# A two-layer mLSTM, GLA and sparse-attention block: matmuls of zeros ahead of the data, a shared first norm, and other buffer counts for the weights

## The chip, the cores and the metric

The kernel runs on one core of a Trainium2 chip. The metric is the device time of one execution in microseconds (us). The engines named below are PE (TensorE, matrix products), DVE (VectorE), ACT (ScalarE), POOL (GpSimd) and SP (SyncE, which here only issues DMAs). PEld is PE's loading of the stationary operand.

## The reference, cut to what matters

One sequence of 512 tokens, width 1024, goes through two layers, all in fp32. A layer normalizes its input, projects it to 9312 columns with one weight matrix, feeds three mixers with the columns, gates their outputs and projects 2048 columns back:

```
p   = split_columns(rmsnorm(x, norm_g) @ w_in)          # [512, 1024] @ [1024, 9312]
hm  = mlstm_chunkwise(silu(conv(p.ml_q, p.ml_k)), p.ml_v, gates) * sigmoid(p.ml_o)
hg  = gla_chunked(p.gla_q, p.gla_k, p.gla_v, decay)     # 4 heads
hd  = dsa_sparse_attention(...)                         # top-128 keys of an index score
y   = concat(norm(hm)*silu(ml_z), norm(hg)*silu(gla_r), hd*silu(dsa_z))
x   = x + y @ w_out                                     # [512, 2048] @ [2048, 1024]
```

Here `rmsnorm(x, g)` is `x * rsqrt(mean(x*x) + 1e-6) * g`.

## The kernel before, in words

**Products in three passes.** Every big product is made of three one-pass matmuls in a rounded fp32 format (fp32r): each operand is split into a high part (rounded) and a low part (the rest), and `mm3` (L516) issues high x high, high x low and low x high. The normalized input is kept as `xhi` and `xlo`, eight tiles of 128 columns for 512 tokens.

**Weights.** The host packs both layers' weights into 178 pieces of 128 x 1024 floats (512 KB), in the order of use. A piece takes three steps: SP loads it as `raw`; ACT copies it to `hi` (fp32r); DVE computes `lo = raw - hi`. All three kinds of tile come from one pool `w` with `W_BUFS` = 11 places, and at most `RAWS` = 3 pieces are loading or unsplit. After the split the raw tile's place is free, so a ready piece holds two places. `make_room` (L460) issues loads, `prepare` (L472) does one step of splitting (first the `lo` of the piece whose `hi` was issued, then the `hi` of the next), and `give_back` (L504) frees a piece that PE has used. A load is booked as landed 4.5 us (`LOAD`) after PE's clock at its issue, and `prepare` does not split a piece whose booked landing lies ahead of that clock. `need` (L488) repeats `prepare` until a piece that is wanted is ready.

**Units.** PE goes through units in a fixed order. A `wide` unit has four pieces and 512 columns: it computes four blocks of 128 tokens, 24 matmuls of 512 columns each (`pn` in the profile). In the first unit of a layer each block `sb` first waits for the norm of its 128 rows of x, and the four blocks run one after another over all four pieces; in other wide units the first two blocks run over all four pieces, and then the last two share each piece. Units `in`, `gqk` and `misc` (two, two and one piece) give transposed results (`pt`); units `out` (four pieces) are the last projection (`pw`).

**Planner.** Each engine runs its instructions in the order in which the program issues them. The order is worked out in Python while the program is built: `Meter` (L164) gives each instruction a cost, `Clock` (L208) keeps a time for each engine, and `Background` (L267) holds generators for all other work (norms, convolutions, scans, attention), each of which yields between steps. After each six or so projection matmuls `tick` (L512) calls `prepare` and then starts steps that are due at PE's clock. These planner times only fix the order; they are no times of the chip.

**The start.** `norm_in` (L614) is the norm of a block of 128 rows: squares and their sum, then two small POOL instructions (`rstd_of`, L412), then the scaled copy `xs` on ACT, then eight transposes on PE in two halves of four (`psx`), after each of which ACT writes four tiles of `xhi` and DVE four tiles of `xlo`. The sum of squares is on DVE for blocks 0, 2 and 3 and on ACT for block 1. The loop after the norm tasks (L657) runs the norm of block 0 by hand: two steps (squares, POOL), `prepare`, one step (`xs`), `prepare`, one step (first half), `prepare`, two steps (second half), `prepare`. PE's planner clock is set to at least 5.0 and 6.5 at the first two.

**Space.** Tiles of 128 x 1024 floats for everything else come from the pool `t4`, with `N_T4` = 11 places.

Of the kernel before, what the change touches and what calls it, by code (L numbers as in the profile page):

```python
# [14 lines left out]
AF = mybir.ActivationFunctionType  # L15
OP = mybir.AluOpType
# [143 lines left out]
def free_size(ap):  # L160
    return math.prod(ap.shape[1:])


class Meter:  # L164


    def __init__(self, engine, name, clock):
        self.engine, self.name, self.clock = engine, name, clock
# [12 lines left out]
    def cost(self, op, args, kw):  # L181
        out = args[0]
        if op == "dma_start":
            return None
        if self.name == "pe":
            if op == "transpose":
                return 0.109
            n, one_pass = free_size(out), kw["rhs"].dtype == F32R
            if one_pass:
                return max(n, 256) / 2210 + 0.002  # L190
            if out.shape[0] == 64:
                return max(n / 950, 0.08)
            return max(4 * n, 256) / 2400 + 0.004
        n = free_size(args[1]) if op == "max" else free_size(out)
        pointers = sum(hasattr(v, "ap") and free_size(v) == 1 for v in (*args[2:], *kw.values()))
        accum = kw.get("accum_out") is not None
        if self.name == "act":
            switch = self.clock.ln != (args[2] == AF.Ln)
            self.clock.ln = args[2] == AF.Ln
            return 0.155 + n / 1138 + 0.09 * pointers + 0.12 * accum + 1.3 * switch  # L200
        if self.name == "dve":
            return 0.15 + n / 945 + 0.06 * min(pointers, 1) + 0.02 * accum
        if kw.get("op") == OP.pow:
            return 0.45 + 0.15 * n
        return 0.1 + n / (510 if op == "tensor_tensor" else 600) + 0.1 * (op == "tensor_tensor")


class Clock:  # L208
# [4 lines left out]
    def __init__(self):  # L213
        self.at = dict(pe=0.0, act=0.0, dve=0.0, pool=0.0, sync=0.0)
        self.now = 0.0
        self.ln = True
        self.written, self.touched = {}, {}
        self.rings = {}

    def begin(self):  # L220
        self.now = self.at["pe"]
# [29 lines left out]
    def book(self, engine, cost, outs, ins):  # L251
        at = self.at
        start = max([at[engine]] + [self.latest(self.written, engine, v) for v in ins]
                    + [self.latest(self.touched, engine, v) for v in outs])
        if cost is None:
            at[engine] = start + self.ISSUE
            end, engine = start + self.DMA, "dma"
        else:
            at[engine] = end = start + cost
        self.now = max(self.now, end)  # L260
        for v in outs:
            self.written.setdefault(v.name, {})[self.box(v)] = end, engine
        for v in outs + ins:
            self.touched.setdefault(v.name, {})[self.box(v)] = end, engine
# [69 lines left out]
def hybrid_kernel(ctx, tc, a, out, dbg=None):  # L334
# [12 lines left out]
            nc.gpsimd.dma_start(dbg[name], ap)  # L347

    ctx.enter_context(tc.manual_schedule())
    N_T4, N_T2 = 11, 19  # L350
    W_BUFS, RAWS, LOAD = 11, 3, 4.5
    const = ctx.enter_context(tc.tile_pool(name="const", bufs=1))
    par = ctx.enter_context(tc.tile_pool(name="par", bufs=2))
    wp = ctx.enter_context(tc.tile_pool(name="wp", bufs=2))
# [6 lines left out]
    def pp(name):  # L361
        t = psp.tile([128, 512], F32, tag="pp", name=name)
        clock.ring("pp", t, 3)
        return t

    def pa(name):
        t = psa.tile([128, 512], F32, tag="pa", name=name)
        clock.ring("pa", t, 5)
        return t

    def t4(name, n=1024, dtype=F32):
        return wk.tile([128, 1024], dtype, tag="t4", name=name, bufs=N_T4)[:, 0:n]
# [4 lines left out]
    def small(name, n=8, bufs=None):  # L377
        return sm.tile([128, n], F32, tag=f"s{n}", name=name, bufs=bufs or {1: 10, 4: 8, 8: 8}[n])

    def blocks(t, b):  # L380
        return t.rearrange("p (b c) -> p b c", b=b)

    xr = const.tile([128, NB, D], F32, name="xr")
# [21 lines left out]
    qzs = [const.tile([128, 2, 64 * NB], F32, name=f"qz{i}") for i in range(2)]  # L405
    for t in qzs:
        for odd, r in enumerate(HALVES):
            nc.gpsimd.memset(t[r, 1 - odd], 0.0)
    lev = const.tile([128, len(LEVELS), 32], U8, name="lev")


    def rstd_of(ss, n, dim, rs, scale=1.0):  # L412
        nc.gpsimd.tensor_scalar(rs, ss, scale / dim, scale * EPS, op0=OP.mult, op1=OP.add)
        nc.gpsimd.tensor_tensor(rs, rs, mhalf[:, :n], op=OP.pow)


    def high_part(ps, hi, gain=None):
        if gain is None:
            nc.scalar.activation(hi, ps, AF.Copy)
        else:  # L420
            for c in range(ps.shape[1]):
                nc.scalar.activation(hi[:, c], ps[:, c], AF.Copy, scale=gain[:, c:c + 1])

    def low_part(ps, hi, lo, gain=None):
        if gain is None:
            nc.vector.tensor_sub(lo, ps, hi.bitcast(F32))
        else:
            for c in range(ps.shape[1]):
                nc.vector.scalar_tensor_tensor(lo[:, c], ps[:, c], gain[:, c:c + 1], hi[:, c].bitcast(F32),
                                               op0=OP.mult, op1=OP.subtract)  # L430
# [16 lines left out]
    units, to_load = [], []  # L447
# [9 lines left out]
    def w_tile(name, dtype):  # L457
        return wp.tile([128, 1024], dtype, tag="w", name=name, bufs=W_BUFS)

    def make_room(most=RAWS):  # L460
        while to_load and state["raw"] < most:
            if state["used"] + 1 > W_BUFS - (2 if any(p.hi is None for p in wanted) or not held else 0):
                break
            p = to_load.pop(0)
            state["used"] += 1
            state["raw"] += 1
            p.raw = w_tile("raw", F32)
            nc.sync.dma_start(p.raw, a["w_pack"][p.layer, p.at])
            p.loaded = clock.at["pe"] + LOAD
            to_split.append(p)  # L470

    def prepare():  # L472
        if half_done:
            p = half_done.pop()
            lo = w_tile("lo", F32R)
            nc.vector.tensor_sub(lo, p.raw, p.hi.bitcast(F32))
            state["used"] -= 1
            state["raw"] -= 1
            p.parts = [[t[:, c:c + p.n] for c in range(0, 1024, p.n)] for t in (p.hi, lo)]
            make_room()  # L480
        if to_split and to_split[0].loaded <= clock.at["pe"] and state["used"] + 2 <= W_BUFS:
            p = to_split.pop(0)
            state["used"] += 2
            p.hi = w_tile("hi", F32R)
            nc.scalar.activation(p.hi, p.raw, AF.Copy)
            half_done.append(p)

    def need(p):  # L488
        while p.parts is None:
            if not half_done:  # L490
                clock.at["pe"] = max(clock.at["pe"], to_split[0].loaded)
            prepare()
        return p.parts
# [16 lines left out]
    bg = Background(clock, N_T2 - 1)  # L510
# [103 lines left out]
    def norm_in(gain, sb, square):  # L614
        xs = t4("xs")
        rs = small("rx", 1)
        if square == "act":
            nc.scalar.activation(xs, xr[:, sb, :], AF.Square, accum_out=rs)
        else:
            nc.vector.tensor_tensor_reduce(xs, xr[:, sb, :], xr[:, sb, :], 1.0, 0.0, op0=OP.mult, op1=OP.add,  # L620
                                           accum_out=rs)
        yield
        rstd_of(rs, 1, D, rs)
        yield
        nc.scalar.activation(xs, xr[:, sb, :], AF.Copy, scale=rs)
        yield
        split = []
        for half in range(2):
            ps = pa("psx")
            for j in range(4):  # L630
                k = 4 * half + j
                nc.tensor.transpose(ps[:, 128 * j:128 * j + 128], xs[:, 128 * k:128 * k + 128], ident)
            d = (slice(None), slice(4 * half, 4 * half + 4), slice(128 * sb, 128 * sb + 128))
            split.append((blocks(ps, 4), xhi[d], xlo[d], gain[:, 4 * half:4 * half + 4]))
            high_part(split[-1][0], split[-1][1], split[-1][3])
            if half:
                low_part(*split[0])
            yield "pe"
        yield
        low_part(*split[1])  # L640
# [6 lines left out]
    params = []  # L647

    def norm_task(layer, sb, ready=0.0):
        return bg.add(norm_in(params[layer][:, 88:96], sb, "act" if sb == 1 else "dve"), "norm", ready)  # L650

    norms = []
    make_room(2)
# [14 lines left out]
    for layer in range(DEPTH):  # L668
# [646 lines left out]
        for n, step in enumerate(PLAN):  # L1315
# [3 lines left out]
            _, name, g0, quarter = step  # L1319
# [32 lines left out]
```

## Time and profile before

| | before |
|---|---|
| time, median of 3 runs | 1228.73 us (1228.69 to 1230.84) |
| profiled execution, its own time | 1227.63 us |
| span of the profiled execution | 1225.9 us |
| PE busy | 1198.3 us (98%) |
| DVE busy | 835.1 us (68%) |
| ACT busy | 600.6 us (49%) |
| POOL busy | 171.0 us (14%) |
| mean granted TensorE clock | 0.996 |
| bytes moved by DMA | 107.70 MB, mean 88 GB/s |

The span runs from the first to the last instruction; the execution's own time is 1.7 us longer. Matmuls overlap in the records: a 512-column fp32r matmul is listed with about 0.40 us, and the next one starts 0.23 us after it. Nearly all instructions stand under line 178, the recorder's call, so rows are told apart by the names of their tiles. The letter q after an engine (SPq) is its instruction queue.

### The profile page before, as it was taken

Reading aid. Unit: us, or ns where it says so; the run is one execution under the profiler, and the core shown is the slowest. Engines: PE = TensorE matmul, PEld = TensorE weight load, DVE = VectorE, ACT = ScalarE, POOL = GpSimd, SP = SyncE. Lnnn points to the kernel's source line nnn. Section 1 sums busy time; section 2 is a strip of 40 time slices with the busy share of each in tenths; the row PEclk is TensorE's granted clock in tenths of the full one; section 3 lists DMA queues with packets and bytes.
Section 4 is the critical chain, followed back from the end, with each engine's and each line's share of the span. In section 5 each row is a group of like instructions: output and inputs, shape, how many; then the busy total and the mean of one; then the engine's idle time right before and its main releaser. Section 6 shows DMA issues by size and latency. Waiting matters only on the chain. (4 is left out here: it accounts for less than half of the span.)

```text
span 1225.9 us, 16513 instructions
## 1 busy us (share of the span) xinstructions
PE 1198.3 (98%) x6004; PEld 970.6 (79%) x6004; DVE 835.1 (68%) x1650; ACT 600.6 (49%) x1334; POOL 171.0 (14%) x309
## 2 busy tenths in 40 slices
PE   6999899999999999999999999999999999999998
PEld 4877687888888887788879777888788888778887
DVE  5477797876777765355555888879867867544644
ACT  6565446554344354652366654474443443555421
POOL 2001221321000010210010023031210000122000
PEclk8999999999999999999999999999999999999999
DMA  5333122212332234132124222222222223233221
GB/s 195 108 98 104 44 92 72 86 61 55 105 108 69 70 119 129 53 112 86 69 70 128 63 86 79 80 73 86 71 70 86 79 85 104 70 112 112 69 82 73
DMA packets 35152, 107.70 MB, mean 88 GB/s; under 512 B 5028, under 2 KB 8388, under 8 KB 35072
## 3 DMA queue, kind: packets, MB, share of 16 engines
q1 hardware_dynamic: 33136, 104.89, 26.5%
q0 software_dynamic: 1200, 1.36, 0.3%
q8 instruction: 47, 0.77, 0.3%
q10 hardware_dynamic: 736, 0.41, 0.1%
q14 instruction: 33, 0.27, 0.1%
HBM read 104.48 MB, written 3.43 MB: 88 GB/s over the span
## 5 line engine op out<-in xcount | busy, mean ns | idle before, releaser
L178 DVE TENSOR_TENSOR lo<-raw,hi 128x1024 fp32r<-128x1024 f32 x178 | 219.1, 1231 | 140.2 <-ACT hi L178 133.5
L178 PE MATMUL pn<-hi,xhi 128*128 128x512 f32 x768 | 313.4, 408 | 0.4 <-ACT xhi L178 0.4
L178 PE MATMUL pn<-lo,xhi 128*128 128x512 f32 x768 | 305.2, 397 | 4.1 <-DVE lo L178 4.1
L178 PE MATMUL pn<-hi,xlo 128*128 128x512 f32 x768 | 304.1, 396 | 0.0
L178 ACT ACTIVATE hi<-raw 128x1024 fp32r<-128x1024 f32 x178 | 188.7, 1060 | 197.9 <-PE pn L178 96.8
L178 PEld LDWEIGHTS pn<-lo,xhi 128*128 128x128 f32 x768 | 145.1, 189 | 37.7 <-DVE lo L178 7.0
L178 PEld LDWEIGHTS pn<-hi,xlo 128*128 128x128 f32 x768 | 144.6, 188 | 35.8 <-DVE xlo L178 1.3
L178 PEld LDWEIGHTS pn<-hi,xhi 128*128 128x128 f32 x768 | 145.1, 189 | 33.2 <-issue 0.8
L178 PE MATMUL pt<-xhi,hi 128*128 128x512 f32 (+1 forms) x400 | 159.1, 398 | 0.0
L178 PE MATMUL pt<-xhi,lo 128*128 128x512 f32 (+1 forms) x400 | 154.6, 387 | 0.0
L178 PE MATMUL pt<-xlo,hi 128*128 128x512 f32 (+1 forms) x400 | 154.5, 386 | 0.0
L178 PE MATMUL pw<-hi,yhi 128*128 128x512 f32 x256 | 102.1, 399 | 0.8 <-DVE zz L178 0.8
L178 PE MATMUL pw<-hi,ylo 128*128 128x512 f32 x256 | 100.0, 391 | 0.0
L178 PE MATMUL pw<-lo,yhi 128*128 128x512 f32 x256 | 99.8, 390 | 0.0
L178 PEld LDWEIGHTS pt<-xhi,hi 128*128 128x128 f32 x400 | 75.2, 188 | 18.0 <-issue 3.9
L178 PEld LDWEIGHTS pt<-xhi,lo 128*128 128x128 f32 x400 | 75.3, 188 | 15.3
L178 PEld LDWEIGHTS pt<-xlo,hi 128*128 128x128 f32 x400 | 75.5, 189 | 12.7
L178 DVE TENSOR_TENSOR xr<-pw,xr 128x512 f32<-128x512 f32 x64 | 44.2, 690 | 58.7 <-PE pw L178 58.7
L178 DVE SCALAR_TENSOR_TENSOR cacc<-cbuf,pv,cacc 128x512 f32<-128x512 f32 x96 | 73.3, 763 | 2.5 <-ACT el L178 0.2
L178 PEld LDWEIGHTS pw<-hi,yhi 128*128 128x128 f32 x256 | 48.1, 188 | 10.5 <-DVE zz L178 1.2
L178 PEld LDWEIGHTS pw<-hi,ylo 128*128 128x128 f32 x256 | 48.0, 188 | 10.3
L178 PEld LDWEIGHTS pw<-lo,yhi 128*128 128x128 f32 x256 | 48.2, 188 | 9.3
(187 smaller groups left out, 1671.0 us busy)
## 6 DMA issues: line engine op xcount, KB each, us to landing
raw<-w_pack SPq DMA_DIRECT2D x178, 512.0 KB, 3.5
xr<-x SPq DMA_DIRECT2D x4, 512.0 KB, 7.3
negm<-negm SPq DMA_DIRECT2D x8, 256.0 KB, 3.7
bs<-skew SPq DMA_DIRECT2D x8, 256.0 KB, 4.0
out_dram<-xr SPq DMA_DIRECT2D x8, 256.0 KB, 2.0
bs<-skew SPq DMA_DIRECT2D x8, 192.0 KB, 4.5
skew<-flat POOLq DMA_DIRECT2D x1, 1280.0 KB, 16.1
bs<-skew SPq DMA_DIRECT2D x8, 128.0 KB, 4.5
```

The source lines that it names most:

```text
L178: return f(*args, **kw)
```

## The change

- Seven matmuls of 256 columns on zeroed data (`qzs[0]`, fp32, 64 rows) are issued to PE before anything else, into a PSUM tile `idle` that nothing reads.
- The norm of block 0 of layer 0 splits the squares: DVE takes columns 0 to 511, ACT columns 512 to 1023, and POOL adds the two sums. The scaled copy `xs` of that block is issued in two halves.
- The `hi` of the very first piece is a DVE copy and no longer an ACT copy.
- The pool `w` has 12 places, at most 2 pieces loading or unsplit; the pool `t4` has 10 places.
- The planner books 0.085 us on PE whenever PE leaves one-pass fp32r matmuls for transposes or other fp32 matmuls.

```diff
             if op == "transpose":
-                return 0.109
+                switch = self.clock.leave()
+                self.clock.projecting = False
+                return 0.109 + switch
             n, one_pass = free_size(out), kw["rhs"].dtype == F32R
+            switch = 0.0 if one_pass else self.clock.leave()
+            self.clock.projecting = one_pass
             if one_pass:
                 return max(n, 256) / 2210 + 0.002
             if out.shape[0] == 64:
-                return max(n / 950, 0.08)
-            return max(4 * n, 256) / 2400 + 0.004
+                return max(n / 950, 0.08) + switch
+            return max(4 * n, 256) / 2400 + 0.004 + switch
...
+        self.projecting = False
...
+    def leave(self):
+        return 0.085 * self.projecting
...
-    N_T4, N_T2 = 11, 19
-    W_BUFS, RAWS, LOAD = 11, 3, 4.5
+    N_T4, N_T2 = 10, 19
+    WARM = 7
+    W_BUFS, RAWS, LOAD = 12, 2, 4.5
...
+    idle = pp("idle")
+    for _ in range(WARM):
+        nc.tensor.matmul(idle[:, 0:256], lhsT=qzs[0][0:64, 1, 0:128], rhs=qzs[0][0:64, 1, :], start=True, stop=True)
...
             p.hi = w_tile("hi", F32R)
-            nc.scalar.activation(p.hi, p.raw, AF.Copy)
+            if p is units[0][1][0]:
+                nc.vector.tensor_copy(p.hi, p.raw)
+            else:
+                nc.scalar.activation(p.hi, p.raw, AF.Copy)
...
-        if square == "act":
+        if square == "both":
+            rs2 = small("rx", 1)
+            l, r = xr[:, sb, 0:512], xr[:, sb, 512:1024]
+            nc.vector.tensor_tensor_reduce(xs[:, 0:512], l, l, 1.0, 0.0, op0=OP.mult, op1=OP.add, accum_out=rs)
+            nc.scalar.activation(xs[:, 512:1024], r, AF.Square, accum_out=rs2)
+            nc.gpsimd.tensor_tensor(rs, rs, rs2, op=OP.add)
+        elif square == "act":
...
-        nc.scalar.activation(xs, xr[:, sb, :], AF.Copy, scale=rs)
+        for c in ((slice(0, 512), slice(512, 1024)) if square == "both" else (slice(0, 1024),)):
+            nc.scalar.activation(xs[:, c], xr[:, sb, c], AF.Copy, scale=rs)
...
-        return bg.add(norm_in(params[layer][:, 88:96], sb, "act" if sb == 1 else "dve"), "norm", ready)
+        return bg.add(norm_in(params[layer][:, 88:96], sb, "act" if sb == 1 else "both" if not (layer or sb) else "dve"), "norm", ready)
```

## Rows read from the trace of the kernel before

**Rows 1.** Page, part 1: engine busy us, share of span, instructions.
```profile
PE 1198.3 (98%) x6004; PEld 970.6 (79%) x6004; DVE 835.1 (68%) x1650; ACT 600.6 (49%) x1334; POOL 171.0 (14%) x309
```
**Rows 2.** Waits of PE: waiter, releaser, us in total, times, longest.
```profile
PE psq L178 <- ACT qn L178: 4.1, 2, 2.2
PE pn L178 <- DVE lo L178: 4.1, 6, 1.9
PE psga L178 <- DVE qz L178: 2.7, 1, 2.7
```
**Rows 3.** Timeline of PE, start: start us, us, engine, line, op, count [idle before].
```profile
8.32 1.97 PE L178 MATMUL psx<-ident,xs 128*128 128x128 f32 x8 [8.32 <-ACT xs L178]
...
12.07 0.42 PE L178 MATMUL pn<-lo,xhi 128*128 128x512 f32 x1
...
16.54 0.40 PE L178 MATMUL pn<-hi,xlo 128*128 128x512 f32 x1
19.80 1.97 PE L178 MATMUL psx<-ident,xs 128*128 128x128 f32 x8 [2.86 <-ACT xs L178]
22.13 0.80 PE L178 MATMUL pn<-hi,xhi 128*128 128x512 f32 x1 [0.36 <-ACT xhi L178]
```
**Rows 4.** Busy time by stretch; the number behind POOL is the granted clock.
```profile
19.80:25.20 5.40, 5.04 (x15) 3.49 (x16) 2.16 (x8) 4.08 (x10) 0.00 (x0) 0.50 0.00 0
```
**Rows 5.** Timeline of DVE, start.
```profile
4.61 1.23 DVE L178 CUSTOM_DVE_ANT_0 xs<-xr 128x1024 f32<-128x1024 f32 x1 [3.44 <-DMA xr<-x]
...
7.26 1.23 DVE L178 TENSOR_TENSOR lo<-raw,hi 128x1024 fp32r<-128x1024 f32 x1 [1.43 <-ACT hi L178]
...
10.65 1.13 DVE L178 SCALAR_TENSOR_TENSOR xlo<-psx,pv,xhi 128x128 fp32r<-128x128 f32 x4 [0.17 <-ACT xhi L178]
...
13.92 1.22 DVE L178 TENSOR_TENSOR lo<-raw,hi 128x1024 fp32r<-128x1024 f32 x1
```
**Rows 6.** Timeline of ACT, start.
```profile
7.13 1.13 ACT L178 ACTIVATE xs<-xr,rx 128x1024 f32<-128x1024 f32 x1
...
9.47 1.14 ACT L178 ACTIVATE xhi<-psx,pv 128x128 fp32r<-128x128 f32 x4 [0.26 <-PE psx L178]
...
14.34 0.24 ACT L178 ACTIVATION_READ_ACCUMULATOR xs<-xr 128x1 f32 x1
17.05 0.85 ACT L178 ACTIVATE zw<-wa 16x256 fp32r<-16x256 f32 x2 [2.47 <-DMA wa<-gla_w_a]
17.91 0.66 ACT L178 ACTIVATE gv<-pn 128x256 f32<-128x256 f32 x2
18.60 3.23 ACT L178 ACTIVATE xs<-xr,rx 128x1024 f32<-128x1024 f32 x3
21.73 2.15 ACT L178 ACTIVATE xhi<-psx,pv 128x128 fp32r<-128x128 f32 x8
...
38.37 1.06 ACT L178 ACTIVATE hi<-raw 128x1024 fp32r<-128x1024 f32 x1 [0.51 <-PE pn L178]
```
**Rows 7.** Timeline of POOL, start.
```profile
1.13 1.33 POOL L178 MEMSET qz<- 64x256 f32 x4
6.02 0.19 POOL L178 TENSOR_SCALAR rx<-rx 128x1 f32<-128x1 f32 x1 [3.56 <-DVE rx L178]
6.29 0.56 POOL L178 TENSOR_TENSOR rx<-rx,mhalf 128x1 f32<-128x1 f32 x1
```
**Rows 8.** Timeline of DVE: a reduction over 512 columns, later in the run.
```profile
488.95 0.69 DVE L178 CUSTOM_DVE_ANT_0 bs<-psl,bs 128x512 f32<-128x512 f32 x1 [5.23 <-POOL bs L178]
```
**Rows 9.** Critical chain: eight fp32 products of 128 columns (16 records).
```profile
1144.84 1.78 PE pod L178 x16
```
**Rows 10.** Timeline of PE: the longest wait for a weight.
```profile
131.91 0.50 PE L178 MATMUL pn<-lo,xhi 128*128 128x512 f32 x1 [1.85 <-DVE lo L178]
```
**Rows 11.** Busy time by stretch, columns as in Rows 4.
```profile
146.00:147.00 1.00, 1.00 (x10) 0.79 (x7) 0.57 (x2) 0.00 (x0) 0.00 (x0) 0.50 0.06 16
494.00:495.00 1.00, 0.58 (x2) 0.28 (x2) 0.00 (x0) 1.00 (x4) 1.00 (x2) 1.00 0.00 0
```

## The prediction

> **What bounds the kernel now.** First the busy shares: PE is busy 98% of the span, every other engine at most 68% [rows 1]. So the time is PE's work plus the stretches in which PE has nothing to do or runs at half rate, and the change can gain only there. Then PE's timeline and its list of waits. At the start PE stands still for 8.32 us, works on the first block of tokens until 16.94, stands still again for 2.86 us and then 0.36 us for the norm of the second block, and gets going at 22.13 [rows 3]; from 19.8 to 25.2 the clock column shows 0.50, the lower of its two levels (1.2 GHz) [rows 4]. All later gaps are small: 4.1 us in six waits for the low part of a weight (the longest 1.85 us), 4.1 us in two waits for the normalized queries and keys, 2.7 us in one wait of the GLA products [rows 2, 10]. The start holds some 11.5 us of idle time, the rest of the run about 12.
>
> **The part that is easy to miss: what the zeros do to the planner.** Seven matmuls go through the recorder, so the planner books them on PE: 0.43 each by the code's formula, from 1.38 (its end of the first memset plus its semaphore cost) to 4.39. The loads of the first four pieces are issued after that in program order, so they are booked as landed at 4.39 + 4.5 = 8.89 instead of 4.5. The four calls of prepare in the start loop come at 5.0, 6.5, about 7.4 and about 8.1 of PE's planner clock (scaled copies booked until 6.77 and 7.47, then two times four transposes), all below 8.89. None of them splits anything; in the kernel before, each did. All splitting starts in need(), after both halves of the first norm. These numbers decide the order only. By them DVE's order becomes: half of the squares, four xlo, hi of piece 0, lo 0, lo 1, four xlo, lo 2, the squares of block 2, lo 3. Before it was: squares, lo 0, lo 1, four xlo, lo 2, four xlo, lo 3, squares of block 2.
>
> **The start in chip time.** The first block of x is usable at 4.61 [rows 5]. DVE's half takes 0.69 as a reduction of 512 columns did [rows 8]; ACT's half I estimate at 0.8, half of 1.13 for 1024 columns plus 0.24 for reading the sum [rows 6]. POOL starts about 0.18 after, as before (5.84 to 6.02), and has three small steps instead of two: 0.27 + 0.27 + 0.56 [rows 7], which ends at 6.7. The first half of xs (0.6) ends at 7.3, the transposes start at 7.4 against 8.32: 0.9 us earlier. The zeros begin behind the first qz memset, at about 1.6 [rows 7]. A 256-column fp32 product costs 0.45 at the full clock (eight of 128 columns took 1.78 [rows 9]) and I estimate 0.9 at the lower level, so seven end between 4.7 and 7.9: in the worst case the transposes start 0.5 late.
>
> Then DVE's chain. Four transposes (0.5 at the full clock, half of 1.97 / 2 [rows 3]) and four xhi (1.14 [rows 6]) put the first xlo at 9.3. From there to the end of lo 3 there are two xlo groups of 1.1, the copy, three lo (0, 1, 2), one squares, and lo 3, each 1.15 to 1.23 [rows 5], and a tiny scale: 2 x 1.1 + 6 x 1.15 + 0.1 = 9.2, so lo 3 ends near 18.5; before it ended at 15.14 [rows 5]. Five matmuls at 0.23 follow, and block 0 ends near 19.75 instead of 16.94: **+2.8**. The hi of piece 0 on DVE does not show in the trace; its bounds are 1.23, the subtraction of the same size, and 0.6, half of it, and I take 1.15 because that row is the nearest. For the copy, the Trainium skill ("VectorE: DVE Perf Modes", The perf-mode tier table) says that an fp32 copy between SBUF tiles runs at twice the rate of a two-input operation. No row here shows one; by that rule the sum of the start would be 0.5 us smaller.
>
> Behind block 0, ACT's order sets when block 1 can begin. Before: zw (which had waited until 17.05 for its DMA), gv, three xs, xhi, and PE's first matmul of block 1 at 22.13, 5.19 after the end of block 0 [rows 3, 6]. After: gv can start at once (-0.85), but with 12 places a fifth piece fits already here (8 held + 2 loading + 2), so its hi (1.06 [rows 6]) goes ahead of the second xs, and zw's 0.85 lands behind it, ahead of the last two xs: about +0.9 in all. So block 1 starts near 25.8: **start +3.7**. Bounds: +2 (short copy, no hi or zw in front) and +5 (block 0's last six matmuls at the lower level, 1.4 more). The zeros do not buy the clock back: PE has little to do from about 8.4 to 11.5 and stands still again before block 1, and a gap of 2.7 us was followed by 0.50 [rows 11] while one of 1.96 was not.
>
> **The weights.** A wide unit holds 8 places. With 11 places and 3 loading nothing more can be split until PE gives the first piece back; with 12 and 2 one piece more is ready. The six waits for lo (4.1 us) are late by 1.85 at most [rows 2, 10], and one piece is at least 24 matmuls x 0.23 = 5.6 us of PE's work: I take all of them as gone, **-4.1**; bounds 0 and -4.1. That a piece loads with one fewer in flight I cost at nothing: DVE's lo hides it, since the next load is issued right there, a piece's worth of work ahead; if that cover went, one wait would cost a landing time.
>
> **The planner's 0.085 and the t4 places.** Both move steps between places, they add no instruction. PE's planner clock runs ahead a little, so steps of ACT and DVE come earlier in program order; the 6.8 us of other waits [rows 2] may shrink or grow. One place fewer in t4 could make a first write wait for the last reader of a place. Cost 0 each; bounds together -4 and +3 (a gap like the longest one more).
>
> **Sum.** Against the profiled execution, 1227.63 (span 1225.9 and 1.7 around it): +3.7 - 4.1 = 1227.2. The median of the runs is 1.1 higher than that execution, so the forecast is **1228.3**, no change that can be measured: a measurement of this kernel can tell about 0.2%, 2.5 us.
>
> **Rivals.**
> *A: the start goes as the words of the change say.* If the splits keep their places in the start loop, DVE copies hi 0 at 6.2, when its raw lands, and its chain ends at 14.0 instead of 15.14; gv's 0.85 less and zw's 0.85 more cancel. Start -1.2, with the weights -5.3: 1223.4. For it: DVE is free from 5.8 to 7.26 [rows 5]. Against it: the planner's 8.89. Chance 0.14.
> *B: the waits in the middle go too.* The GLA wait (2.7) drags a stretch at 0.50 behind it [rows 11], some 3.3 us, so 1.65 more, and the queries and keys cost 4.1 [rows 2]. If half of these 8.4 go: 1228.3 - 4.2 = 1224.1. For it: the planner now knows what leaving the projections costs. Against it: these waits are for DVE and ACT, which the new term does not slow down in its books, so it asks for their results earlier. Chance 0.18.
> *C: slower, because DVE and not the number of places makes lo late.* All six waits are ended by DVE's lo, none by ACT's hi or a load [rows 2, 10]. One more piece split ahead is 1.23 us of DVE work earlier, which pushes the convolutions and the GLA products back by as much, and PE waits there instead. Then the 4.1 stay as other waits and the start's +3.7 stands: 1232.0. It decides as soon as less than 1.2 us of the waits is saved. Chance 0.26.
> The forecast has 0.42, and 1225.8 to 1230.8 for its own range.
>
> **How the numbers follow.** The likeliest case gives the time. Faster by over 0.2%: A, B and a twentieth from the forecast's tail, less a little of B that stays within, 0.35. Slower: most of C and a little of the tail, 0.26. Within: 0.39. The range goes from the far side of A and B, 1222.5, to 1233.0, C with one more microsecond.
>
> **What would show it.** In the profile after: zeros on PE from about 1.6; transposes near 7.4; DVE's lo of piece 0 after the first xlo and lo 3 near 18.5; block 1's first pn near 25.8 (right) or below 21.5 (A). In the list of PE's waits, lo near 0 and psga and psq about as before. The prediction is wrong if block 1 starts before 22.13, if lo still stands at 4 us (C), or if the wait for psga is gone (B).

## The result, and the profile after

The changed kernel takes **1219.13 us** (median of 4 runs, 1218.32 to 1220.31) against 1229.47 for the kernel before in the same session: ratio 0.9915, 95% interval 0.9898 to 0.9933. The prediction was no measurable change (1228.3, range 1222.5 to 1233.0), so it was too slow by 9.2 us. The profiled execution takes 1219.62 with a span of 1217.7, 8.2 us below the span before.

The page's first part after, to hold against [rows 1]:

```profile
PE 1202.5 (99%) x6018; PEld 976.6 (80%) x6018; DVE 832.8 (68%) x1651; ACT 600.2 (49%) x1336; POOL 169.3 (14%) x310
```

PE's waits after (waiter, releaser, us in total, times, longest), to hold against [rows 2]:

```profile
PE psx L178 <- ACT xs L178: 2.7, 1, 2.7
PE pn L178 <- DVE hi L178: 2.2, 1, 2.2
PE pn L178 <- ACT xhi L178: 2.2, 1, 2.2
PE idle L178 <- POOL qz L178: 1.5, 1, 1.5
PE psga L178 <- DVE qz L178: 1.1, 1, 1.1
PE pn L178 <- DVE lo L178: 0.9, 2, 0.5
```

Here idle are the zeros, psx the norm's transposes, pn matmuls of a projection, psga the GLA products, psq the transposes of the normalized queries and keys. The first four lines are all of the start, and so are 0.4 of the 0.9 us for lo (the row at 13.13 below). Of the rest of the run, psq has left the list (4.1 before), lo went from 4.1 to 0.5, psga from 2.7 to 1.1.

PE's timeline at the start, to hold against [rows 3]:

```profile
1.49 6.34 PE L178 MATMUL idle<-qz 64*128 64x256 f32 x14 [1.49 <-POOL qz L178]
7.76 1.97 PE L178 MATMUL psx<-ident,xs 128*128 128x128 f32 x8
11.96 0.77 PE L178 MATMUL pn<-hi,xhi 128*128 128x512 f32 x1 [2.23 <-DVE hi L178]
13.13 0.80 PE L178 MATMUL pn<-lo,xhi 128*128 128x512 f32 x1 [0.40 <-DVE lo L178]
...
20.58 0.40 PE L178 MATMUL pn<-hi,xlo 128*128 128x512 f32 x1
23.70 1.10 PE L178 MATMUL psx<-ident,xs 128*128 128x128 f32 x8 [2.73 <-ACT xs L178]
27.04 0.79 PE L178 MATMUL pn<-hi,xhi 128*128 128x512 f32 x1 [2.23 <-ACT xhi L178]
```

Block 0's last matmul starts at 20.58 (16.54 before), block 1's first at 27.04 (22.13 before). DVE and ACT of the same stretch, to hold against [rows 5, 6]:

```profile
4.62 0.69 DVE L178 CUSTOM_DVE_ANT_0 xs<-xr 128x512 f32<-128x512 f32 x1 [3.45 <-DMA xr<-x]
...
11.13 0.68 DVE L178 CAST hi<-raw 128x1024 fp32r<-128x1024 f32 x1
11.85 2.36 DVE L178 TENSOR_TENSOR lo<-raw,hi 128x1024 fp32r<-128x1024 f32 x2
...
17.50 1.22 DVE L178 TENSOR_TENSOR lo<-raw,hi 128x1024 fp32r<-128x1024 f32 x1
...
21.01 0.66 ACT L178 ACTIVATE gv<-pn 128x256 f32<-128x256 f32 x2 [6.05 <-PE pn L178]
21.56 1.06 ACT L178 ACTIVATE hi<-raw 128x1024 fp32r<-128x1024 f32 x1
22.50 1.15 ACT L178 ACTIVATE xs<-xr,rx 128x1024 f32<-128x1024 f32 x1
23.68 0.84 ACT L178 ACTIVATE zw<-wa 16x256 fp32r<-16x256 f32 x2
```

Where the time went: I matched each projection matmul on PE with the same one before and subtracted start times. The changed kernel is 5.4 us **behind** from the second block up to 124 us of the run before, level at 340 us, 2.6 ahead at 530, 4.8 at 780, 5.9 at 1034 and 8.2 at the end. So the start lost 5.4 us, and the rest won 13.6.

### The profile page after: what moved, and what is told of

It reads as the page before. It is cut to its first block, busy times and chain, and to the rows that moved or that the text cites. A ratio compares the mean times of both kernels' runs of the same rounds, so it can differ in the third digit from the quotient of the medians.

```text
span 1217.7 us, 16527 instructions
## 1 busy us (share of the span) xinstructions
PE 1202.5 (99%) x6018; PEld 976.6 (80%) x6018; DVE 832.8 (68%) x1651; ACT 600.2 (49%) x1336; POOL 169.3 (14%) x310
## 4 chain that ended last, share of the span: by engine, by line
PE 88%; DVE 1%; issue 0%; ACT 0%; ACTq 0%
PE pn L178 42%; PE pt L178 17%; PE pw L178 14%; PE psS L178 2%; PE pom L178 2%; PE psga L178 1%; PE pod L178 1%; PE psl L178 1%; PE pog L178 1%; PE psy L178 1%; PE pst L178 1%; PE pss L178 1%; PE psq L178 1%; PE psx L178 0%; PE psst L178 0%; DVE lo L178 0%
```

## The experiments

Ratios are to the kernel before; "12/2" means 12 places, two loading.

**The start.** Three ways to take the start's loss away, each from the changed kernel: the start of before; the zeros issued past the recorder, so that the planner does not book them; no zeros.

```diff
 e3: no zeros, norm of block 0 as "dve", hi of piece 0 on ACT
 e4: -nc.tensor.matmul(idle...)   +bass_nc.tensor.matmul(idle...)
 e5: -WARM = 7   +WARM = 0
```

> The changed kernel with the start of before: no zeros, the first norm on DVE alone, the first hi on ACT; the places and the booked 0.085 stay. Theory S (the start of the changed kernel loses 5 us and the middle wins 13): block 1 starts near 22 us, time 1213 to 1215. Rival (the middle only came out well because the start was late): block 1 at 22 us, but middle waits back, time 1219 or more.

> The changed kernel, but the seven matmuls of zeros are issued past the planner, which books nothing for them; so the first pieces count as landed at 4.5 again and are split inside the start loop. Theory S (it is the booking that makes the start late): lo of piece 3 ends near 14.5, block 1 starts near 21 us instead of 27, time 1212 to 1214. Rival (the zeros themselves or the clock make it late): block 1 starts after 25 us, time 1217 to 1220.

> The changed kernel without the seven matmuls of zeros (their count set to 0); shared norm, hi 0 on DVE, places and 0.085 stay. Theory N (the zeros gain nothing: in the run with unbooked zeros all seven ran at the lower clock level and the transposes after them too): time within 1.5 us of the run with unbooked zeros (1213.3), full rate reached at about 11.5 us all the same. Rival (zeros shorten the stretch at the lower level): 1.5 to 3 us slower than the run with unbooked zeros, 1215 to 1216.

Measured: e3 1211.94 us (ratio 0.9875, 0.9860 to 0.9890), e4 1213.26 (0.9882, 0.9865 to 0.9898), e5 1213.09 (0.9875, 0.9859 to 0.9890). All three beat the changed kernel by 6 to 7 us. Matched matmul by matmul, e3 runs 8.0 us ahead of the changed kernel from 49 us on and 8.1 at the end: the difference is made in the start and nowhere else. e4 keeps every zero and loses only their booking (its block 1 starts at 22.70 us, not near 21 as I had expected). So it is the booking that costs; the work of the zeros itself costs and gives little.

The same edit alone, on the kernel before:

```diff
 e6: kernel before + zeros, norm on two engines, hi of piece 0 on DVE
```

> The kernel before with the start of the changed kernel alone: seven booked zeros, shared norm, hi 0 on DVE; 11 places, 3 loading, 11 in t4, no 0.085. Theory S: block 1 starts 3.5 to 4.5 us later than before (no fifth weight in front with 11 places), middle waits as before, time 1231 to 1234. Rival (the start helps by setting the planner's PE clock right): middle waits shrink, time 1224 to 1229.

Measured: 1233.75 us, ratio 1.0043 (1.0027 to 1.0060). The start alone makes the kernel slower, by 5 us.

**The middle: each edit taken back, each edit alone.**

```diff
 e1: changed kernel,  -return 0.085 * self.projecting   +return 0.0
 e2: changed kernel,  W_BUFS 12 -> 11, RAWS 2 -> 3, N_T4 10 -> 11
 e7: kernel before + the booked 0.085
 e8: kernel before + W_BUFS 12, RAWS 2, N_T4 10
```

> The changed kernel, but the planner books nothing for leaving the projections (0.085 set to 0); zeros, shared norm, 12 places and 2 loading stay. Theory P (the 12 places took the middle waits away): waits of PE after 100 us stay near 2.3 us in total, time within 2 us of the changed kernel's 1219. Theory L (the booked 0.085 did it): the waits of before come back, 10 to 12 us of them, time 1227 to 1232. Block 1 starts at 27 us under both.

> The changed kernel with 11 places for weights, 3 loading, and 11 places in t4 as before; zeros, shared norm and the booked 0.085 stay. Theory P: the waits for lo come back (about 4 us in total) and with them others, time 1225 to 1232. Theory L: lo waits at most 4 us back, the waits for queries and keys (4.1 before) and for the GLA products (2.7 before) stay away, time 1219 to 1223. Block 1 starts 1 us earlier than in the changed kernel (no fifth weight ahead of the second xs).

> The kernel before with nothing but the booked 0.085. Theory P and L together (each helps by itself): 1222 to 1226. Theory X (the 0.085 helps only with the 12 places; alone it makes PE ask earlier for results of ACT and DVE): waits for queries and keys grow from 4.1 to 6 or 7 us, time 1230 to 1234.

> The kernel before with nothing but 12 places for weights, 2 loading, and 10 places in t4. Theory P: lo waits below 1 us, psq waits gone, GLA waits 4 to 5 us in total; time 1217 to 1220, that is e1_no_leave minus its late start. Rival (most of the middle's gain needs the 0.085): 1224 to 1228.

Measured: e1 1225.67 (0.9978, 0.9968 to 0.9987), e2 1236.61 (1.0073, 1.0058 to 1.0088), e7 1227.18 (0.9995, 0.9982 to 1.0007), e8 1222.13 (0.9939, 0.9920 to 0.9957). Neither theory of e1 holds as written: its time lies between the two, and of the waits only psga came back (5.3 us). The new start and the 0.085 with the old places (e2) lose 8.3 us, with 7.2 us of psq. Alone, the 0.085 gives nothing that can be told from zero (in e7 theory X had the waits right and the time wrong) and the places give 6.2 us; together (e3) they give 16.4. PE's waits say why. With the 0.085 alone (e7), then with the places alone (e8), then with both (e3):

```profile
PE psq L178 <- ACT qn L178: 5.9, 3, 3.0
PE pn L178 <- DVE lo L178: 3.8, 5, 1.8
```

```profile
PE psga L178 <- DVE qz L178: 7.0, 4, 3.1
...
PE pn L178 <- DVE lo L178: 0.5, 1, 0.5
```

```profile
PE psga L178 <- DVE qz L178: 1.1, 1, 1.1
...
PE pn L178 <- DVE lo L178: 0.5, 1, 0.5
```

The 0.085 removes psga and leaves psq and lo; the places remove psq and lo and let psga grow; only both take all three to 1.1 us or less. How the 0.085 does it stands in PE's order. First the places alone (e8), then the changed kernel (left out between its rows are projection matmuls):

```profile
144.91 1.12 PE L178 MATMUL psga<-qz,dec 128*64 128x64 f32 x16 [3.05 <-DVE qz L178]
145.97 2.58 PE L178 MATMUL psS<-ml_q,ml_k 128*128 128x512 f32 x6
```

```profile
142.67 0.69 PE L178 MATMUL psga<-qz,dec 128*64 128x64 f32 x16 [1.12 <-DVE qz L178]
...
148.99 1.55 PE L178 MATMUL psS<-ml_q,ml_k 128*128 128x512 f32 x6
...
151.78 1.22 PE L178 MATMUL psS<-ml_q,ml_k 128*128 128x384 f32 x6
152.94 0.69 PE L178 MATMUL psga<-qz,dec 128*64 128x64 f32 x16
```

Without the 0.085 the second group of GLA products stands ahead of the mLSTM products psS and waits 3.05 us; with it, two groups of psS stand first, and the GLA products find their data ready. The order of these groups in e3, which differs from e8 in the 0.085 alone, is that of the changed kernel. The waiting group and the one behind it also run at half rate (16 products in 1.12 against 0.69; six of psS in 2.58 against 1.55): the mean granted clock of 130 to 150 us is 0.91 in e8 and 1.00 in e3.

A larger value, on e3:

```diff
 e11: e3 with 0.085 -> 0.17
```

> e3_old_start with 0.17 booked for leaving the projections instead of 0.085. Theory T (the more PE time is booked, the later in PE's order the dependent products stand, so the waits go): GLA waits 0 to 1.1 us, time 1211 to 1213. Theory O (0.085 happens to give a good order, and any other value moves the steps to other places): waits of 3 us or more come back somewhere in the middle, 1214 to 1222.

Measured: 1219.06 (0.9921, 0.9906 to 0.9936), 7 us worse than e3, with 1.8 us of waits of the attention's transposes and 1.5 of psq. So 0.085 is not the start of a trend; it moves the order, and 0.17 gives another order. The waits that are new on the list are half of the 7 us (3.6); the other half is not traced.

**Which number of places?** My first theory (K) was that a ready piece more is what counts.

```diff
 e9:  e3 with RAWS 2 -> 3      (12/3)
 e10: e3 with W_BUFS 12 -> 11  (11/2)
```

> The run with the start of before, 12 places and 0.085 (e3_old_start, 1211.9), but 3 pieces loading instead of 2. So 12 places hold 4 ready pieces and 3 raw ones in a wide unit, and one place is left over that no split fits into. Theory K (what counts is the number of ready pieces, five instead of four): the waits for lo and for queries and keys come back, 1220 to 1228. Rival (what counts is the number of places as such): 1211 to 1214.

> e3_old_start with 11 places and 2 loading. In a wide unit 8 places are held and 2 are raw, so one place is left and a split needs two: four ready pieces again. Theory K: like e9_three_loading, 1220 to 1228. Rival (fewer pieces loading is the point, since ACT and DVE split them later): 1211 to 1214.

Measured: 12/3 1213.43 (0.9874, 0.9859 to 0.9889), 11/2 1211.02 (0.9853, 0.9837 to 0.9870), beside 1211.94 for 12/2. Each gets there without the other change: 11/2 without the twelfth place, 12/3 with three pieces loading. Only the pair 11 and 3 has the waits of psq. Theory K fell for the time and for psq; on lo it had a part, for lo waits 1.7 us in both runs, against 0.5 in e3 and 3.8 in e7. Why 12/3 and 11/2 have less of it than 11/3 is not shown. 11/2 with the start of before is the fastest version I ran, 8.1 us below the changed kernel by the medians.

**Why 11/3 makes the queries late.** The rows of the attention's bias (`bs<-skew`) are issued by SP in order, behind weight loads that wait for a place. SP in the kernel before, then in the changed kernel:

```profile
474.37 9.50 SPq L178 DMA_DIRECT2D raw<-w_pack  x4
483.97 3.71 SPq L178 DMA_DIRECT2D bs<-skew  x8
```

```profile
474.05 6.37 SPq L178 DMA_DIRECT2D raw<-w_pack  x3
480.52 2.76 SPq L178 DMA_DIRECT2D bs<-skew  x6
```

Before, four loads stand ahead of the rows, some 3 us apart; after, three. POOL adds a mask to them, eight times, and the queries' scale (`rq`) stands behind these additions on POOL. With the 0.085 alone, SP, then POOL:

```profile
481.00 3.71 SPq L178 DMA_DIRECT2D bs<-skew  x8
```

```profile
484.96 6.06 POOL L178 TENSOR_TENSOR bs<-bs,sel 128x512 f32<-128x512 f32 x8 [27.93 <-DMA bs<-skew]
491.10 0.19 POOL L178 TENSOR_SCALAR rq<-rq 128x4 f32<-128x4 f32 x1
```

POOL had waited 27.93 us for these rows. Counted in PE's projection matmuls, SP issues them after matmul 1672 in the kernel before, e2, e7 and e15, all with 11/3, and after 1658, 1658, 1658, 1659 and 1647 in the changed kernel, e3, e8, e9 and e10; PE's transposes psq stand behind matmul 1692 in all of them. The 13 or 14 matmuls (25 in e10) are 3 us or more. The test takes only the rows out of SP's queue:

```diff
 e18: e7 with -nc.sync.dma_start(bs[hh], ...)   +the same DMA from ACT's queue, booked on SP as before
 e15: e7 with N_T4 11 -> 10
```

> Before with the booked 0.085 (11 places, 3 loading), and the bias rows bs<-skew issued from ACT's queue instead of SP's; the planner books them as before, so PE's, DVE's and POOL's order is that of the run with 0.085 alone (1227.18, psq waits 5.9 us, lo waits 3.8). Theory Q (with 11 places and 3 loading SP always stands at a load that waits for a place, the bias rows behind it come late, at 481 us, and with them POOL's eight additions and the scale factor of the queries behind them): POOL's additions start before 478 instead of 484.96, the waits of psq fall from 5.9 to under 2 us, and the time is 1222 to 1224.5. Theory O (the order in which the planner puts the queries' steps makes them late, whenever the rows come): psq stays at 4 us or more and the time is 1226 to 1229, or more where ACT now waits for a place of bs.

> Before with the booked 0.085 and t4 at 10 places instead of 11, weights at 11 places and 3 loading. If t4 has no part in the result: 1227.2, within 1225.5 to 1229, psq waits near 5.9 us, as with 0.085 alone. If the place taken from t4 is what removes the waits for the normalized queries and keys (all runs without these waits had 10): psq below 1 us and 1221 to 1223.

Measured: e18 **1221.98** (0.9938, 0.9921 to 0.9954), 5.2 us below e7; e15 1228.72 (0.9999, 0.9988 to 1.0010), no effect. In e18, ACT's queue, then POOL, then PE's wait:

```profile
477.96 0.35 ACTq L178 DMA_DIRECT2D bs<-skew  x1
```

```profile
481.85 6.06 POOL L178 TENSOR_TENSOR bs<-bs,sel 128x512 f32<-128x512 f32 x8 [24.66 <-DMA bs<-skew]
```

```profile
PE psq L178 <- ACT qn L178: 0.8, 1, 0.8
```

The rows come 3.0 us earlier, everything behind them too, and 5.9 us of psq become 0.8. The order on PE, DVE, ACT and POOL is the same in both runs, and the waits for lo stay at 3.8 us, so it is not that the weights come earlier. Matched with e7, PE is level up to that place (0.2), 5.5 ahead behind it, and 8.4 ahead behind the same place of the second layer (e7's profiled execution was 3.0 us above its median, so the medians differ by less). Some 3.4 of the 5.5 are clock: the mean granted clock of 492.0 to 498.9 us is 0.51 in e7, and of 485 to 500 us 1.00 in e18. Theory Q holds. (POOL's additions began at 481.85, where I had written "before 478"; 3 us earlier was enough.) The places for t4 have no part with 11/3 (e15); with 12/2 that was not tested.

**The clock at the start.** Three single runs with the matmuls on another operand, not booked, as in e4; POOL fills the operand first, so they begin 1.5 us later.

```diff
 e12: ones on 64 rows    e13: zeros on 128 rows    e14: ones on 128 rows
```

> After with the seven matmuls on ones instead of zeros, on the same 64 rows (POOL first fills them with 1.0, for this run alone). Theory V (the values decide: zeros do not count as work): the granted clock rises while they run, as in the run with ones on 128 rows, where seven took 5.12 us. Theory R (the rows decide: half of the array does not count): all seven at about 0.9 us, 6.3 us in all, clock 0.50 until 11 us. The total stays near 1214.8 to 1219 either way.

> After with the seven matmuls on zeros, on 128 rows instead of 64. Theory R (the rows decide): the granted clock rises while they run, seven in about 5.1 us. Theory V (the values decide): all seven at about 0.9 us, 6.3 us in all, clock 0.50 until 11 us. The total stays near 1214.8 to 1219 either way.

> The run with unbooked zeros (e4_unbooked), but the seven matmuls take ones instead of zeros and 128 rows instead of 64 (from a part of xlo that is overwritten later). Theory D (zeros, or half of the rows, do not count as work for the clock): the matmuls start at 0.89 us apart, drop to 0.45 within the seven, and the transposes of block 0 take 0.11 each instead of 0.25. Rival (the clock does not depend on what is in the operands): as before, seven at 0.89 and the transposes at 0.25.

Measured: 1213.79, 1215.09 and 1214.76 us. PE's first two groups in e12, e13 and e14:

```profile
2.98 6.34 PE L422 MATMUL idle<-xlo 64*128 64x256 f32 x14 [2.98 <-POOL xlo L420]
9.25 1.97 PE L178 MATMUL psx<-ident,xs 128*128 128x128 f32 x8
```

```profile
3.00 5.35 PE L422 MATMUL idle<-xlo 128*128 128x256 f32 x14 [3.00 <-POOL xlo L420]
8.19 1.04 PE L178 MATMUL psx<-ident,xs 128*128 128x128 f32 x8
```

```profile
2.99 5.12 PE L422 MATMUL idle<-xlo 128*128 128x256 f32 x14 [2.99 <-POOL xlo L420]
7.95 1.08 PE L178 MATMUL psx<-ident,xs 128*128 128x128 f32 x8
```

The rows made the difference, not the values: on 64 rows, ones as zeros, all seven run at 0.9 us each and the transposes behind them still at the lower level (1.97 for eight); on 128 rows, zeros as ones, the level rises before they end (1.04). All six profiles with 64 rows show the first, both with 128 rows the second. Theory R holds in these runs. Yet the total gains nothing over e4's 1213.26, for block 1 waits for its own norm either way:

```profile
19.76 1.42 PE L178 MATMUL psx<-ident,xs 128*128 128x128 f32 x8 [3.37 <-ACT xs L178]
```

In e14 that is 3.37 us; in e4, whose first block runs slower, it is 3.16 and PE goes on at 19.81.

## Why the prediction was wrong

**The start: right in cause and order, a third too small.** The order of DVE's instructions came out as written, from the booked zeros: half squares, four xlo, hi, lo, lo, four xlo, lo, squares, lo. e4 shows that the booking is the cause. Predicted transposes at 7.4, measured 7.76 (the zeros ended at 7.8, the upper end of what I gave); block 1 begins 6.06 us after block 0's end, predicted 6.05. The lo of piece 3 ends at 18.72, predicted 18.5, but that is partly luck: the first xlo came at 10.09 and not 9.3, as the transposes began 0.4 later and took 1.97 us, not half of it, while the copy of hi took 0.68 and not 1.15. The 0.68 is against 1.22 for a subtraction of the same size, 1.8 times its rate. The Trainium skill ("VectorE: DVE Perf Modes", The perf-mode tier table) gives an fp32 copy in SBUF twice the rate of a two-input operation; the trace nearly agrees, and I should have taken that. The size that was missed is block 0's end: 20.98 and not 19.75, +4.0 and not +2.8, since its matmuls ran at the lower level until 17.98 (0.43 apart), so PE and not lo 3 ended the block; I had this only as a bound. That puts block 1's start at +4.9 against +3.7. Block 1 then ran at the lower level until 31.7 us, 4.7 us long, where before it had done so for 3.7 (until 25.8), which makes +5.4. By itself this would have made the result slower than forecast, and it hid a part of the error in the middle.

**The weights' places: near on lo, and blind to the rest.** Behind the start lo went from 4.1 to 0.5, so 3.6 of the predicted 4.1 came. My reason, one more ready piece, explains at most a part (11/2 does as well in time and has 1.7 of lo), and I priced the places by lo alone. They also freed SP's queue: the bias rows behind a waiting load came 3 us earlier, and psq's 4.1 us went, a gain that the sum had at nothing. I had followed the loads to the pieces and not to what else SP issues behind them.

**The failed step: "The planner's 0.085 and the t4 places ... Cost 0 each".** For t4 nothing speaks against it (e15, tested with 11/3 only). For the 0.085 it was wrong: with the new places it takes psga from 5.3 us (e1) to 1.1, and with it the stretch at half rate behind one of these waits. e1 prices it: taking it back costs 6.5 us. With the old places it is worth nothing (e7), so the zero was wrong only beside the other edit. With psq above, these are the terms that the sum had at nothing: the rest of the run won 13.6, and the forecast had 4.1. Rival B named the mechanism (the half-rate stretch behind psga, the queries) but took half of it, 4.2, with 0.18, and psq went by the places and not by the 0.085, as B had it; the whole of its 8.4 would have given 1219.9, near the result (1221.6 with the start's true cost). My argument against B, that the planner would only ask earlier for the results of DVE and ACT, was wrong because PE's own order also moved: other products now stand ahead of the ones that waited. Rival C fell for the changed kernel, where psga is 1.1 and not 2.7 plus 1.2; with the places alone (e8) waits for DVE did take the place of lo, 7.0 us of them, though whether from DVE's earlier splits or from the order is not separated.

**The sum.** The start lost 5.4 us and the rest won 13.6. Waits that are gone from the rest: lo 3.6, psq 4.1, psga 1.6, and the wait of the out projection for zz (0.75 before), 10.0 in all. The stretch at half rate behind psga gives 1.8 more: the granted clock of 130 to 150 us, the number behind POOL, before and after:

```profile
130.00:150.00 20.00, 15.45 (x85) 12.03 (x85) 15.21 (x23) 5.48 (x12) 5.27 (x10) 0.91 0.12 41
```

```profile
130.00:150.00 20.00, 18.40 (x95) 14.10 (x94) 17.98 (x27) 9.88 (x19) 4.16 (x9) 1.00 0.21 67
```

It is the only such stretch before: from 30 to 140 and from 150 to 1220 us the clock is 1.00. A wait also costs about 0.16 us more than the list says, since a matmul is listed with 0.39 and the next one otherwise starts 0.23 behind it; for the eight waits that are gone I estimate 1.3. That is 13.1 of 13.6; the rest is not traced.

## What to carry to other kernels

A matmul that only warms the engine should not be booked without looking at what a planner then reorders: here its booking cost 6 us, and its work brought nothing. When an edit changes how full a queue of loads is, follow everything else that the same engine issues behind those loads, to the engine that uses it. A change with two edits to the order can be worth more than its parts, as each alone may give its gain back in the wait that the other removes; so a planner's constant that moves the order has the waits near it as its bound, and not zero as its price.

## What the hardware showed that I had not expected

- The seven zeros on 64 rows kept PE busy for 6.34 us without the clock rising; on 128 rows it rose within 5.35. The column of the granted clock shows 1.00 there all the same (3 to 5 us, changed kernel, next row; the number behind POOL), so at the start the level is read from durations, not from that column.

```profile
3.00:5.00 2.00, 2.00 (x6) 1.60 (x5) 0.39 (x1) 0.39 (x1) 0.00 (x0) 1.00 1.04 407
```

- Gaps of like length went differently: PE stood still for 3.18 us before block 1 in e3 and the granted clock stayed at 1.00 (first fence), for 3.16 us in e4 and it was 0.50 from 19 to 25 us (second). Nor is a threshold to be read from shorter gaps: behind a wait of 1.85 us for lo the clock was 0.50 in e7 (133.7 to 137.0 us) and stayed at 1.00 in the kernel before (131 to 140 us). Why, these runs don't tell.

```profile
19.50:25.00 5.50, 4.92 (x28) 3.85 (x29) 2.21 (x9) 5.50 (x17) 0.74 (x2) 1.00 0.18 72
```

```profile
19.00:25.00 6.00, 5.04 (x18) 4.11 (x19) 3.31 (x11) 5.00 (x14) 2.35 (x4) 0.50 0.21 82
```

- DVE's two products into qz take 0.85 us when POOL is idle and 1.69 while POOL multiplies dec beside them (e8, DVE twice, then POOL). That is part of the 3.05 us wait of psga there.

```profile
135.79 0.85 DVE L178 TENSOR_TENSOR qz<-dec,gq 64x256 f32<-64x256 f32 x2
...
143.08 1.69 DVE L178 TENSOR_TENSOR qz<-dec,gq 64x256 f32<-64x256 f32 x2
```

```profile
142.85 1.63 POOL L178 TENSOR_TENSOR dec<-ta 128x256 f32<-128x256 f32 x2
```
